# Last 256 tokens as transposed 32x32 blocks, scaled by two engines; the first norm's sums two products later

## The chip, the cores and the metric

The kernel runs on one core of one Trainium2 chip. Time is the device time in microseconds (us) of one execution; lower is better. The core's engines work side by side and wait for each other through semaphores: TensorE (PE, matrix products into PSUM banks), VectorE (DVE), ScalarE (ACT), GpSimd (POOL, hardly used here) and SyncE (SP), whose queue issues the loads and stores.

## What is computed

One decoder layer in fp32 for 1024 tokens of width 1024, then a last norm. Cut to what this change touches:

```python
def rms_norm(x, g):
    xf = x.astype(jnp.float32)
    y = xf * lax.rsqrt(jnp.mean(xf * xf, axis=-1, keepdims=True) + RMS_EPS)
    return (y * g.astype(jnp.float32)).astype(x.dtype)
...
        z = rms_norm(h, norm_mix_g[l])
        proj = z @ w_in[l]
        ...                       # pooling heads, gated recurrence, output projection, MLP
        z = rms_norm(h, norm_ple_g[l])
        gate = jax.nn.sigmoid(z @ w_ple_gate[l] + b_ple_gate[l])
        h = h + gate * (p[l] @ w_ple_proj[l])
    return rms_norm(h, norm_final_g)
```

The output is (1, 1024, 1024).

## The kernel before

Everything lies transposed: 128 of the 1024 channels on the partitions, tokens along the free dimension. `H[0]` to `H[7]` are the eight channel tiles of the residual stream (128 x 1024), `T[0]` to `T[5]` six spare tiles of that size, `R` the inverse root of a norm. A product in fp32 is made of three fp32r products of split operands (high x high, high x low, low x high; helper `mm`, L350), each over at most 512 tokens. A PSUM bank holds 512 columns; there are two pairs of banks and four single ones.

A norm's mean is a sum over channels, that is over partitions: ACT squares each tile, DVE adds the squares up, and PE multiplies them by a matrix of ones (`n_ps`, "the sums", L416 and L417 with split operands `hl`, L426 unsplit). Each row of the result is the same; DVE transposes it in 32x32 blocks so that each of a few columns holds 128 different tokens, ACT takes the root of these columns (`edge`, L438), DVE the reciprocal, and a second transpose of the broadcast columns brings it back to one value a column (L434 to L440, `Norm.rstd`).

The first projection (`ps_l`, three output tiles) goes over the eight input tiles k as they arrive; the norm's factor is multiplied in afterwards, at the eviction (L535). At the last k, the sums of the first norm are placed ahead of that tile's three groups of products. Behind it the loop over the other input projections (`ps_i`), gates (`ps_g`, L571, whose evictions are ACT's L579), pooling and recurrence begins.

At the end comes the gated per-layer input. It goes in four groups of tokens: 0 to 511, 512 to 1023 for channel tiles 2 to 5, then 512 to 767 and 768 to 1023 for the tiles 6, 7, 0, 1. For each channel tile PE makes the gate product (`ps_e`, 24 products) and the projection (`ps_j`, 6); DVE multiplies the gate by `R` (L1045), ACT takes the sigmoid (L1046), DVE multiplies by `ps_j` (L1051) and adds to `H` (L1052); ACT squares the new tile (L389), DVE adds it to the running sum (L390), and ACT multiplies the tile by the last norm's gain (L1081). Tokens 0 to 767 are scaled and stored while products still run (L1071, L1061). For the last 256, the last tile's chain is: gate, sigmoid, product, add, square (L1153), sums, transpose, root, reciprocal, transpose, and then four products of two tiles by the broadcast factor (L1093), each followed by its store (L1094).

The order of work is that of the code as a scheduler places it by its own estimate of times; `pin` (while `in_order` is set) holds an instruction at its place in program order. SP's queue is in order too.

Of the kernel before, what the change touches and what calls it, by code (L numbers as in the profile page):

```python
# [11 lines left out]
ALU = mybir.AluOpType  # L12
# [46 lines left out]
def block_kernel(  # L59
# [65 lines left out]
    def bank(name):  # L125
        return pd.tile([P, HALF], F32, tag="pd", name=name)
# [248 lines left out]
    class Norm:  # L375
# [43 lines left out]
                parts.append((hs, o))  # L419
            return parts  # L420

        def sums_of(self, hs, squares):

            o = bank(f"{self.name}_ps{hs.start}")[:, : hs.stop - hs.start]
            for n, sq in enumerate(squares):
                nc.tensor.matmul(o, ones_f, sq, start=n == 0, stop=n == len(squares) - 1)  # L426
            return [(hs, o)]

        def rstd(self, out, parts=None):


# [92 lines left out]

# [487 lines left out]

    fin = Norm("n3", T[0], T[1:3])
    rfin = T[5]
    gate_p, held, squares = {}, [], [T[0][:, GROUPS[-1]]]
    root = pool.tile([P, 1], F32, name="root")

    def ple_psum(g, hs, o, apart):
# [23 lines left out]
    def ple_out(hs, o, pg, pj, add=True, then=None):  # L1042
        t = T[3 + o % 2][:, : hs.stop - hs.start]
        hv = H[o][:, hs]
        nc.vector.tensor_tensor(by(t, pg), got(pg), by(R[:, hs], pg), ALU.mult)  # L1045
        pin(nc.scalar.activation(t, t, AF.Sigmoid, bias=col("b_ple", o)))  # L1046
        e = t
        if then:
            then(t)
            e = T[3 + (o + 1) % 2][:, : hs.stop - hs.start]  # L1050
        nc.vector.tensor_tensor(by(e, pj), by(t, pj), got(pj), ALU.mult)  # L1051
        nc.vector.tensor_tensor(hv, hv, e, ALU.add)  # L1052
# [27 lines left out]
    def gain(o, hs):  # L1080
        return nc.scalar.activation(H[o][:, hs], H[o][:, hs], AF.Identity, scale=col("g_fin", o))  # L1081

    def finish_last(hs, end, squares):

        fin.rstd(rfin, fin.sums_of(hs, squares))
        gain(end, hs)
        n = hs.stop - hs.start
        done = t_all[:, 1:3].rearrange("p a s -> p (a s)")[:, : NT * n].rearrange("p (o s) -> p o s", o=NT)
        r = rfin[:, hs].unsqueeze(1).broadcast_to([P, 2, n])
        low = end // 2 * 2  # L1090
        for o in [*(o for o in range(0, NT, 2) if o != low), low]:
            os = slice(o, o + 2)
            nc.vector.tensor_tensor(done[:, os], h_all[:, os, hs], r, ALU.mult)  # L1093
            nc.sync.dma_start(out_end[:, os], done[:, os])  # L1094

    END = len(GROUPS) - 1
    for g, hs in enumerate(GROUPS):
        last = len(ORDER[g]) - 1
        if g == END:
            fin.n[hs.start] = len(ORDER[1])  # L1100
        for n, o in enumerate(ORDER[g]):
            end = g == END and n == last
            pg, pj = ple_psum(g, hs, o, end)
            if g == 0 and n < 2:
                ple_gate(g, hs, o, pg, n == 1)
                held.append((o, pg, pj))
                if n == 0:
                    first_sums()
                    continue
                for o, pg, pj in held:  # L1110
                    ple_proj(hs, o, pj)
                for o, pg, pj in held:
                    ple_out(hs, o, pg, pj)
            elif end:
                ple_gate(g, hs, o, pg)
                ple_proj(hs, o, pj)
            else:
                ple_proj(hs, o, pj)
                ple_gate(g, hs, o, pg)
            if g == 0 and 1 <= n < 5:  # L1120
                raw = wp.tile([P, S], F32, tag="raw", name=f"wg0_{n + 3}_raw")
                nc.sync.dma_start(raw, w_gate[n + 3])
                split(raw, *B[n + 3])
                gate_p[n + 3] = B[n + 3]

            if (g > 0 or n > 1) and not end:
                ple_out(hs, o, pg, pj, g < END or n < last - 1)
            if g == 0 and n > 0:
                for o in LATER[n - 1]:
                    ple_in(o, SECOND, norm2)  # L1130
                if n == NT - 2:
                    norm2.rstd(R, norm2.sums((SECOND,)))
            if g == 1:
                gain(o, hs)
                finish(FIRST, DONE[n])
            if g == END - 1:
                gain(o, hs)
            if g == END and n < last - 1:
                gain(o, hs)
            if end:  # L1140
                prev = ORDER[g][n - 1]
                sqs = [T[1 + i][:, hs] for i in range(2)]

                def between(t):

                    pin(nc.scalar.activation(sqs[0], H[prev][:, hs], AF.Square))
                    pin(nc.scalar.activation(root, t[:, :1], AF.Sqrt))
                    pin(gain(prev, hs))

                in_order[:] = [True]  # L1150
                ple_out(hs, o, pg, pj, False, between)
                in_order.clear()
                nc.vector.tensor_tensor(sqs[1], H[o][:, hs], H[o][:, hs], ALU.mult)  # L1153
                squares += sqs
            if g == END:
                finish(GROUPS[END - 1], LAST[n])
    finish_last(GROUPS[-1], ORDER[-1][-1], squares)
    leave("ple")
    leave("proj")

# [72 lines left out]
```

## Time and profile before

| | us |
|---|---|
| median of 3 runs | 927.12 (926.88 to 928.76) |
| profiled execution, its time | 927.23 |
| its span, first to last instruction | 925.4 |
| PE busy | 915.3 (99%) |
| DVE busy | 758.8 (82%) |
| ACT busy | 456.5 (49%) |
| granted PE clock, mean | 0.998 |

In the profile's rows L with a number is a line of the kernel; `out<-in` are the program's names, with buffer numbers left out. PEld is PE's weight load, which runs beside its products. In a list by time a row has its start from the span's first instruction, its length, engine, line, operation, shape and count, and in brackets how long the engine was idle before it and what ended that. Rows of equal instructions that follow each other are merged, and an instruction may start up to 0.1 us before the end of the one ahead when it doesn't need its result.

### The profile page before, as it was taken

The numbers are of one execution on the slowest core, as the hardware profiler recorded it, in microseconds if no ns is written. First come the engines' busy times: TensorE is split into PE (matmuls) and PEld (weight loads), VectorE is DVE, ScalarE is ACT, GpSimd is POOL, SyncE is SP. The second block draws the span as 40 slices with busy tenths as digits, with TensorE's granted clock in tenths as the row PEclk, the third lists the DMA queues.
The fourth block names the chain that finished last, engine by engine and source line by source line (L and its number), as shares of the span: only waits on it lengthen the run. The fifth ranks groups of instructions, "written<-read, shape, count | busy, mean of one in ns | idle before, by whom it ended". The sixth has DMA issues, their size and how long they took to land.

```text
span 925.4 us, 11180 instructions
## 1 busy us (share of the span) xinstructions
PE 915.3 (99%) x4351; PEld 798.5 (86%) x4351; DVE 758.8 (82%) x903; ACT 456.5 (49%) x531; POOL 5.6 (1%) x7
## 2 busy tenths in 40 slices
PE   9999999999999999999999999999999999999996
PEld 7888888888888888888888888888888888888895
DVE  7997985659998888888888989979776679885676
ACT  7567893447543343344334654443444347652544
POOL 0000000002000000000000000000000000000000
PEclk9999999999999999999999999999999999999999
DMA  7210143211244345344534989366532341031022
GB/s 265 99 47 23 46 151 122 69 45 54 84 175 178 125 161 197 142 138 173 191 125 148 341 317 342 110 202 208 188 111 92 118 156 45 16 122 46 1 91 91
DMA packets 45044, 123.97 MB, mean 134 GB/s; under 512 B 4160, under 2 KB 6208, under 8 KB 44992
## 3 DMA queue, kind: packets, MB, share of 16 engines
q1 hardware_dynamic: 44848, 123.22, 38.3%
q8 instruction: 34, 0.56, 0.3%
q14 instruction: 18, 0.15, 0.0%
q10 hardware_dynamic: 144, 0.04, 0.0%
HBM read 89.69 MB, written 33.55 MB: 133 GB/s over the span
## 4 chain that ended last, share of the span: by engine, by line
PE 95%; DVE 2%; issue 1%; DMA 1%; SPq 0%; ACT 0%; DVEq 0%
PE ps_P_d L350 31%; PE ps_P_u L350 31%; PE ps_i L350 10%; PE ps_e L350 10%; PE ps_o L350 9%; PE ps_j L350 1%; DMA h<-in_xT 1%; PE ps_g L571 1%; PE ps_p L350 1%; DVE t L390 1%; PE ps_l L350 0%; DVE wl_lo L179 0%; PE n_ps L417 0%; DVE t L1093 0%; DVE a L182 0%
## 5 line engine op out<-in xcount | busy, mean ns | idle before, releaser
L350 PE MATMUL ps_P_d<-a,wd_P_hi 128*128 128x512 f32 x880 | 261.7, 379 | 0.0
L350 PEld LDWEIGHTS ps_P_d<-a,wd_P_hi 128*128 128x128 f32 x880 | 166.3, 189 | 23.6
L350 PE MATMUL ps_P_d<-a,wd_P_lo 128*128 128x512 f32 x440 | 166.8, 379 | 0.0
L350 PE MATMUL ps_P_u<-a,wu_hi 128*128 128x512 f32 x512 | 152.3, 379 | 0.0
L350 PE MATMUL ps_P_u<-y,wu_hi 128*128 128x512 f32 x384 | 114.2, 379 | 0.0
L350 PEld LDWEIGHTS ps_P_u<-a,wu_hi 128*128 128x128 f32 x512 | 96.8, 189 | 13.8
L350 PE MATMUL ps_P_u<-a,wu_lo 128*128 128x512 f32 x256 | 97.0, 379 | 0.0
L350 PEld LDWEIGHTS ps_P_d<-a,wd_P_lo 128*128 128x128 f32 x440 | 83.2, 189 | 11.8
L350 PEld LDWEIGHTS ps_P_u<-y,wu_hi 128*128 128x128 f32 x384 | 72.6, 189 | 10.4
L747 DVE TENSOR_TENSOR t<-t,ps_P_u 128x512 f32<-128x512 f32 (+1 forms) x80 | 62.6, 782 | 20.4 <-PE ps_P_u L350 20.4
L350 PE MATMUL ps_i<-a,wi_hi 128*128 128x512 f32 x288 | 74.3, 380 | 0.0
L350 PE MATMUL ps_P_u<-y,wu_lo 128*128 128x512 f32 x192 | 72.8, 379 | 0.0
L178 ACT ACTIVATE a<-wd 128x1024 fp32r<-128x1024 f32 x56 | 58.9, 1054 | 21.4 <-PE ps_P_d L350 11.6
L179 DVE TENSOR_TENSOR a<-wd,a 128x1024 fp32r<-128x1024 f32 x56 | 67.2, 1221 | 1.0 <-ACT a L178 0.6
L350 PE MATMUL ps_o<-y,wo_hi 128*128 128x512 f32 x256 | 65.7, 379 | 0.0
L350 PEld LDWEIGHTS ps_i<-a,wi_hi 128*128 128x128 f32 x288 | 54.1, 189 | 8.8 <-issue 1.0
L178 ACT ACTIVATE wu_hi<-wu 128x1024 fp32r<-128x1024 f32 x24 | 25.4, 1057 | 69.8 <-PE ps_P_u L350 44.2
L178 ACT ACTIVATE wu_hi<-wu_raw 128x1024 fp32r<-128x1024 f32 (+1 forms) x26 | 25.2, 974 | 66.3 <-PE ps_P_u L350 41.3
L350 PEld LDWEIGHTS ps_o<-y,wo_hi 128*128 128x128 f32 x256 | 48.4, 189 | 6.8
L350 PEld LDWEIGHTS ps_P_u<-a,wu_lo 128*128 128x128 f32 x256 | 48.4, 189 | 6.8
L178 ACT ACTIVATE wd_P_hi<-wd 128x1024 fp32r<-128x1024 f32 x24 | 25.3, 1054 | 46.9 <-PE ps_P_d L350 46.8
L389 ACT ACTIVATE t<-h 128x512 f32<-128x512 f32 (+2 forms) x44 | 32.0, 731 | 28.3 <-DVE h L1052 20.5
(223 smaller groups left out, 1502.8 us busy)
## 6 DMA issues: line engine op xcount, KB each, us to landing
wd<-act SPq DMA_DIRECT2D x56, 512.0 KB, 5.7
act<-t SPq DMA_DIRECT2D x32, 512.0 KB, 4.3
wu_raw<-in_w_up SPq DMA_DIRECT2D x16, 512.0 KB, 3.4
wu<-in_w_up SPq DMA_DIRECT2D x16, 512.0 KB, 3.9
act<-wu SPq DMA_DIRECT2D x16, 512.0 KB, 4.6
wd<-in_w_down SPq DMA_DIRECT2D x16, 512.0 KB, 6.2
h<-in_xT SPq DMA_DIRECT2D x14, 512.0 KB, 4.4
wg_raw<-in_w_gate SPq DMA_DIRECT2D x10, 512.0 KB, 3.2
```

The source lines that it names most:

```text
L178: first = pin(nc.scalar.activation(hi, src, AF.Copy))
L179: lowest[:] = [pin((eng or nc.vector).tensor_tensor(lo, src, f32(hi), ALU.subtract)).ins]
L350: ins = nc.tensor.matmul(ps, w, turns(z[:, hs]), start=first and z is zhi and w is whi, stop=last and w is wlo, skip_group_check=more,)
L389: pin(nc.scalar.activation(sq, t[:, hs], AF.Square))
L390: self.eng.tensor_tensor(self.acc[:, hs], self.acc[:, hs], sq, ALU.add)
L571: nc.tensor.matmul(x, w[r, o * P : (o + 1) * P], turns(z[r, at : at + HALF]), start=n == 0, stop=n == 2)
L747: (eng or nc.vector).tensor_tensor(to, to if y is None else y, x, ALU.add)
```

## The change

Three things change.

1. **First norm's sums.** At the last input tile, the sums and what follows them stand between the second and the third output tile's products instead of ahead of the first's.
2. **Layout of the last 256 tokens' output.** Instead of multiplying each tile by a factor that differs by column, each tile (already multiplied by the gain) is transposed on DVE in 32x32 blocks, with all tiles' blocks of the same 32 tokens side by side (`turned`). Then a token is a partition within a block, its factor one value a partition, and one instruction scales 32 tokens of all eight tiles (128 x 256). DVE scales blocks 0, 2, 4, 5 and 7, ACT 1, 3 and 6. The second transpose of the factor goes. The host puts the output's blocks back in order when it reshapes. The spare tiles of the squares move from `T[1:3]` to `T[3:5]`, since `T[1]` and `T[2]` now hold the blocks.
3. **The last tile's chain.** From the add on it goes in halves of 128 tokens, with a bank of sums each; the sums of the earlier tiles are made ahead. ACT's square and gain of the tile before stand ahead of the last sigmoid, not behind it. The four stores carry two blocks each, 128 x 512 as before.

The core of the diff:

```diff
-        if k == NT - 1:
-            norm.rstd(R)
...
         for o in range(3):
+            if k == NT - 1 and o == 2:
+                norm.rstd(R)
             mm(ps_l[o], kblk(whi, o), kblk(wlo, o), *A[k], False, k == NT - 1)
...
-    out_end = out[:, NT * S - n_end :].rearrange("p (o s) -> p o s", o=NT)
+    out_end = out[:, NT * S - n_end :].rearrange("p (b x) -> p b x", b=n_end // S * 4)
+    turned_all = t_all[:, 1:3].rearrange("p a s -> p (a s)").rearrange("p (b o j) -> p b o j", o=NT, j=32)
+    turned_flat = t_all[:, 1:3].rearrange("p a s -> p (a s)").rearrange("p (b x) -> p b x", x=32 * NT)
...
-    def finish_last(hs, end, squares):
-
-        fin.rstd(rfin, fin.sums_of(hs, squares))
-        gain(end, hs)
...
-        for o in [*(o for o in range(0, NT, 2) if o != low), low]:
-            os = slice(o, o + 2)
-            nc.vector.tensor_tensor(done[:, os], h_all[:, os, hs], r, ALU.mult)
-            nc.sync.dma_start(out_end[:, os], done[:, os])
+    def turned(o, src=None):
+        src = H[o][:, GROUPS[-1]] if src is None else src
+        return nc.vector.transpose(turned_all[:, :, o], src)
+
+    def ple_last(hs, prev, o, pg, pj):
...
+        in_order[:] = [True]
+        pin(nc.scalar.activation(before, H[prev][:, hs], AF.Square))
+        pin(gain(prev, hs))
+        pin(nc.vector.tensor_tensor(by(t, pg), got(pg), by(R[:, hs], pg), ALU.mult))
+        pin(nc.scalar.activation(t, t, AF.Sigmoid, bias=col("b_ple", o)))
+        pin(nc.scalar.activation(root, t[:, :1], AF.Sqrt))
+        pin(turned(prev))
+        pin(nc.vector.tensor_tensor(by(e, pj), by(t, pj), got(pj), ALU.mult))
+        sums = [bank(f"n3_ps{hs.start}_{i}")[:, :m] for i in range(2)]
+        for x, cut in zip(sums, cuts):
+            for i, sq in enumerate((T[0][:, hs], before)):
+                nc.tensor.matmul(x, ones_f, sq[:, cut], start=i == 0, stop=False)
+        for x, cut in zip(sums, cuts):
+            pin(nc.vector.tensor_tensor(hv[:, cut], hv[:, cut], e[:, cut], ALU.add))
+            pin(nc.vector.tensor_tensor(own[:, cut], hv[:, cut], hv[:, cut], ALU.mult))
+            nc.tensor.matmul(x, ones_f, own[:, cut], start=False, stop=True)
+        pin(nc.scalar.activation(scaled, hv, AF.Identity, scale=col("g_fin", o)))
...
+        def roots(i):
+            r = rfin[:, hs][:, cuts[i]]
+            pin(nc.vector.transpose(r, sums[i]))
+            x = few[:, 4 * i : 4 * i + 4]
+            pin(nc.scalar.activation(x, r.rearrange("p (b t) -> p b t", t=32)[:, :, 0], AF.Sqrt, bias=eps, scale=1.0 / D))
+            return x
...
+        def on_act(b):
+            x = turned_flat[:, b]
+            pin(nc.scalar.activation(x, x, AF.Identity, scale=few[:, b : b + 1]))
+
+        def on_dve(b):
+            x = turned_flat[:, b]
+            pin(nc.vector.tensor_scalar_mul(x, x, few[:, b : b + 1]))
...
+        a = roots(0)
+        pin(turned(o, scaled))
+        inverse(a)
+        on_dve(0)
+        on_act(1)
+        leave_for(slice(0, 2))
+        b = roots(1)
+        on_dve(2)
+        on_act(3)
+        leave_for(slice(2, 4))
+        inverse(b)
+        on_act(6)
+        on_dve(4)
+        on_dve(5)
+        leave_for(slice(4, 6))
+        on_dve(7)
+        leave_for(slice(6, 8))
...
+        if g == 1:
+            fin.tmp = T[3:5]
...
             if g == END - 1:
                 gain(o, hs)
+                turned(ORDER[1][n])
             if g == END and n < last - 1:
                 gain(o, hs)
+                turned(o)
```

**The new order at three places.** A row is the line, the operation, what it writes and reads, and the shape of what it writes.

PE at the first norm, before (`n0_ps` are its sums, `ps_l0` to `ps_l2` the three output tiles at the last input tile):

```order
L350 MATMUL ps_l2_150<-a_70,wl6_lo_379 128x512 x2
L416 MATMUL n0_ps0_420<-hl0_135,ones_142 128x512
L417 MATMUL n0_ps0_420<-hl0_135,ones_142 128x512
L416 MATMUL n0_ps512_425<-hl1_136,ones_142 128x512
L417 MATMUL n0_ps512_425<-hl1_136,ones_142 128x512
L350 MATMUL ps_l0_147<-a_70,wl7_hi_407 128x512 x4
L350 MATMUL ps_l0_147<-a_70,wl7_lo_408 128x512 x2
```

PE there, changed:

```order
L350 MATMUL ps_l1_0_148<-a_70,wl7_lo_408 128x512
L350 MATMUL ps_l1_512_149<-a_70,wl7_lo_408 128x512
L416 MATMUL n0_ps0_432<-hl0_135,ones_142 128x512
L417 MATMUL n0_ps0_432<-hl0_135,ones_142 128x512
L416 MATMUL n0_ps512_437<-hl1_136,ones_142 128x512
L417 MATMUL n0_ps512_437<-hl1_136,ones_142 128x512
L350 MATMUL ps_l2_150<-a_70,wl7_hi_407 128x512 x4
L350 MATMUL ps_l2_150<-a_70,wl7_lo_408 128x512 x2
L350 MATMUL ps_i0_0_486<-a_70,wi0_hi_415 128x512
```

The twelve products of `ps_l0` and `ps_l1` now go first; on DVE the split `wi_lo` moves ahead of the two transposes of the sums.

DVE some 35 us later, in the first pool window (`recip_t` marks its small steps; `y_114` is the low part of the split whose high part ACT makes from the finished window), before:

```order
L622 COPY t<-t 128x1
L631 SCALAR_TENSOR_TENSOR t<-t 128x1023
L179 TENSOR_TENSOR y_131<-h,y_130 128x1024
L629 TENSOR_TENSOR t<-t,recip_t 128x1
L582 TENSOR_TENSOR h<-h 128x1024
L630 TENSOR_TENSOR t<-t 128x1
L179 TENSOR_TENSOR y_114<-t,y_113 128x1024
```

DVE there, changed:

```order
L615 COPY t<-t 128x1
L179 TENSOR_TENSOR y_131<-h,y_130 128x1024
L622 TENSOR_TENSOR t<-t,recip_t 128x1
L624 SCALAR_TENSOR_TENSOR t<-t 128x1023
L623 TENSOR_TENSOR t<-t 128x1
L575 TENSOR_TENSOR h<-h 128x1024
L179 TENSOR_TENSOR y_114<-t,y_113 128x1024
```

The window's last small step (L630, now L623) stands ahead of the product `h<-h` instead of behind it. On ACT one eviction of the gates (64 x 512) moves ahead of a split's high part a little later.

DVE at the end of the program, before:

```order
L1045 TENSOR_TENSOR t<-ps_e_1_6780,rstd 128x256
L1051 TENSOR_TENSOR t<-t,ps_j_1_6781 128x256
L1052 TENSOR_TENSOR h<-h,t 128x256
L1153 TENSOR_TENSOR t<-h 128x256
L434 STREAM_TRANSPOSE t<-n_ps_6820 128x256
L439 RECIPROCAL edge<-edge 128x8
L440 STREAM_TRANSPOSE t<-edge 128x256
L1093 TENSOR_TENSOR t<-h,t 128x512 x4
```

DVE there, changed, from the second half's square on:

```order
L1101 TENSOR_TENSOR t<-h 128x128
L1109 STREAM_TRANSPOSE t<-n_ps_0_6825 128x128
L1076 STREAM_TRANSPOSE t<-t 128x8x32
L1115 RECIPROCAL edge<-edge 128x4
L1123 TENSOR_SCALAR t<-t,edge 128x256
L1109 STREAM_TRANSPOSE t<-n_ps_1_6826 128x128
L1123 TENSOR_SCALAR t<-t,edge 128x256
L1115 RECIPROCAL edge<-edge 128x4
L1123 TENSOR_SCALAR t<-t,edge 128x256 x3
```

The transpose of the broadcast factor and the four products of 512 columns are gone; a transpose into blocks (128x8x32) and five scaled blocks stand there. Ahead of these rows the add and the square stand twice, for 128 columns each, and a block transpose of the tile before follows the last gate eviction.

More of the change, by code (lines that the diff above doesn't have):

```diff
@@ L1040, in ple_proj, with ple_out @@
             mm([(hs, pj)], kblk(wh, o), kblk(wl, o), hi, lo, k == 0, k == len(ple) - 1)
-    def ple_out(hs, o, pg, pj, add=True, then=None):
+    def ple_out(hs, o, pg, pj, add=True):
         t = T[3 + o % 2][:, : hs.stop - hs.start]
@@ L1046, in ple_out @@
         pin(nc.scalar.activation(t, t, AF.Sigmoid, bias=col("b_ple", o)))
[L1047 to L1052, printed above, removed]
+        nc.vector.tensor_tensor(by(t, pj), by(t, pj), got(pj), ALU.mult)
+        nc.vector.tensor_tensor(hv, hv, t, ALU.add)
         if add:
@@ L1081, in gain, with inverse, leave_for @@
         return nc.scalar.activation(H[o][:, hs], H[o][:, hs], AF.Identity, scale=col("g_fin", o))
[L1083 to L1086 removed]
+    def turned(o, src=None):
+        src = H[o][:, GROUPS[-1]] if src is None else src
+        return nc.vector.transpose(turned_all[:, :, o], src)
+    def ple_last(hs, prev, o, pg, pj):
         n = hs.stop - hs.start
[L1088 to L1094 removed]
+        m = n // 2
+        t, e = (T[3 + i % 2][:, :n] for i in (o, o + 1))
+        before, own = (T[3 + i][:, HALF : HALF + n] for i in range(2))
+        scaled = T[3][:, HALF + n :][:, :n]
+        hv = H[o][:, hs]
+        cuts = slice(0, m), slice(m, n)
+        in_order[:] = [True]
[15 more added lines that the diff above has]
+        pin(nc.scalar.activation(scaled, hv, AF.Identity, scale=col("g_fin", o)))
+        few = spread[:, 16:24]
+        def roots(i):
[4 more added lines that the diff above has]
+            return x
+        def inverse(x):
+            pin(nc.vector.reciprocal(x, x))
+        def on_act(b):
[4 more added lines that the diff above has]
+            pin(nc.vector.tensor_scalar_mul(x, x, few[:, b : b + 1]))
+        def leave_for(bs):
+            nc.sync.dma_start(out_end[:, bs], turned_flat[:, bs])
+        a = roots(0)
[15 more added lines that the diff above has]
+        leave_for(slice(6, 8))
+        in_order.clear()
@@ L1137, in block_kernel @@
                 gain(o, hs)
+                turned(ORDER[1][n])
             if g == END and n < last - 1:
                 gain(o, hs)
+                turned(o)
             if end:
[L1141 to L1154, printed above, removed]
+                ple_last(hs, ORDER[g][n - 1], o, pg, pj)
             if g == END:
                 finish(GROUPS[END - 1], LAST[n])
-    finish_last(GROUPS[-1], ORDER[-1][-1], squares)
     leave("ple")
@@ L1230 @@
     out = np.split(np.asarray(r.results[0]["out"]), [NT * GROUPS[-1].start], axis=1)
-    out = np.concatenate([a.reshape(P, NT, -1) for a in out], axis=2)
+    most, end = out[0].reshape(P, NT, -1), out[1].reshape(P // 32, 32, -1, NT, 32)
+    out = np.concatenate([most, end.transpose(0, 4, 3, 2, 1).reshape(P, NT, -1)], axis=2)
     return c(out.transpose(2, 1, 0)).reshape(1, S, D)
```

7 lines of the change are left out of this document (1 added, 6 removed).

## Prediction

> **What bounds the kernel now.** I read the page's shares first, then what TensorE (PE) waited for, then the places of those waits in order of time. In the view of waits a row is: who waited, for whom, microseconds in total, times, longest.
>
> ```profile
> PE 915.3 (99%) x4351; PEld 798.5 (86%) x4351; DVE 758.8 (82%) x903; ACT 456.5 (49%) x531; POOL 5.6 (1%) x7
> ...
> PE ps_l L487 <- DVE heat L367: 1.1, 1, 1.1
> PE n_ps L416 <- DVE hl L414: 0.6, 1, 0.6
> PE n_ps L417 <- DVE hl L415: 0.4, 1, 0.4
> PE n_ps L426 <- DVE t L1153: 0.4, 1, 0.4
> PE n_ps L426 <- ACT t L1146: 0.3, 1, 0.3
> ```
>
> PE is busy 915.3 of 925.4 us and waits, over the whole program, only in three places: at the start, at the sums of the first norm (`n_ps` on L416 and L417), and at the sums of the last 256 tokens (L426). So time can come from two things alone: PE's stall at the first norm, and the tail in which PE has nothing left to do. The change touches exactly these.
>
> **The first norm's sums.** PE in order of time there (start, length, instruction, count, idle before), then VectorE (DVE):
>
> ```profile
> 31.79 1.03 PE L350 MATMUL ps_l<-a,wl_hi 128*128 128x512 f32 x4
> 32.66 0.59 PE L350 MATMUL ps_l<-a,wl_lo 128*128 128x512 f32 x2
> 33.80 0.49 PE L416 MATMUL n_ps<-hl,ones 128*128 128x512 f32 x1 [0.55 <-DVE hl L414]
> 34.74 0.50 PE L417 MATMUL n_ps<-hl,ones 128*128 128x512 f32 x1 [0.44 <-DVE hl L415]
> ...
> 35.68 1.02 PE L350 MATMUL ps_l<-a,wl_hi 128*128 128x512 f32 x4
> ...
> 39.56 1.03 PE L350 MATMUL ps_i<-a,wi_hi 128*128 128x512 f32 x4
> ```
> ```profile
> 34.00 1.29 DVE L415 TENSOR_TENSOR hl<-t,hl 128x512 fp32r<-128x512 f32 x2
> ...
> 35.92 1.18 DVE L179 TENSOR_TENSOR wi_lo<-wi_raw,wi_hi 128x1024 fp32r<-128x1024 f32 x1
> 37.02 0.71 DVE L434 STREAM_TRANSPOSE rstd<-n_ps 128x512 f32<-128x512 f32 x1
> ```
>
> Four products from 31.79 reach 32.66, so one takes 0.217 of PE's time; the two from 32.66 free it at 33.09. The next product of the projection starts at 35.68: the four sums cost 2.59 us. What they cost when nothing is late stands in the chain at a later norm:
>
> ```profile
> 854.67 0.24 PE n2b_ps L416
> 854.91 0.23 PE n2b_ps L417
> ```
>
> That is 0.47 for a half, 0.94 for both, and the stall is worth 2.59 - 0.94 = 1.65 (the 0.55 + 0.44 shown as idle is less, because a stopped stream also loses the overlap of one product's end with the next). In the new order twelve products (`ps_l` 0 and 1, 12 x 0.217 = 2.60) go ahead of the sums, so PE asks for the operands at 33.09 + 2.60 = 35.69. DVE has the last of them at 34.00 + 1.29 = 35.29. No wait is left: gain 1.65.
>
> What is late next? The sums' last result is there at about 35.69 + 3 x 0.235 + 0.50 = 36.90. DVE now does `wi_lo` (1.18) first, from 35.27, then both transposes, and has read the second bank at 37.1 + 0.71 = 37.8. `ps_i` takes those banks, and PE now arrives at 39.56 - 1.65 = 37.91: in time by 0.1. Behind it DVE's first evictions come 0.3 to 0.5 later than now, because ScalarE's (ACT) root waits for the sums, while PE runs 1.65 earlier. Over the next 80 us I looked for the smallest distance between a producer and PE:
>
> ```profile
> 73.33 1.23 DVE L179 TENSOR_TENSOR y<-t,y 128x1024 fp32r<-128x1024 f32 x1 [1.12 <-ACT y L178]
> 80.71 1.06 ACT L178 ACTIVATE y<-t 128x1024 fp32r<-128x1024 f32 x1 [2.81 <-DVE t L630]
> 81.79 1.25 ACT L579 ACTIVATE h<-ps_g,vecs 64x512 f32<-64x512 f32 x2
> ...
> 108.12 1.28 DVE L535 TENSOR_TENSOR t<-ps_i,rstd 128x512 f32<-128x512 f32 x2
> 109.47 1.56 PE L571 MATMUL ps_g<-y,hl 64*128 64x512 f32 x12
> ```
>
> The closest place is the gates at 109.47: the third product (109.8) takes a bank that DVE has just emptied at 108.12 + 1.28 = 109.40, 0.4 before it. If DVE came no earlier, only 0.4 of the 1.65 would be left. But DVE does come earlier: in the new order the 1.2 us product `h<-h` stands between the pool's last small step and the split that waits for ACT, so the idle 1.12 at 73.33 goes (DVE from 0.4 late to 0.7 early); ACT's wait of 2.81 at 80.71 then ends 0.7 earlier and takes in one of the two gate evictions (1.25 / 2 = 0.62) that now follow it. From there both engines are some 1.3 earlier, DVE empties the bank at about 108.1, and PE asks at 109.8 - 1.65 = 108.15. I take off 0.1: **first term -1.55**, bounds -1.65 and -0.4. Later work is released by PE's own products, so the gain stays.
>
> **The tail.** The chain in order of time (start, length), with its last links (between 916.32 and 917.25 stand the add and the square of the last tile, L1052 and L1153, of one length):
>
> ```profile
> 914.86 0.44 DVE t L1045
> ...
> 915.32 0.52 ACT t L1046
> ...
> 916.32 0.43 DVE h L1052
> ...
> 917.25 0.71 PE n_ps L426 x2
> ...
> 917.99 0.46 DVE t L434
> ...
> 918.47 0.32 ACT edge L438
> ...
> 918.81 0.21 DVE edge L439
> ...
> 919.05 0.46 DVE t L440
> ...
> 919.53 0.69 DVE t L1093
> ```
>
> The first store goes out when the first of four DVE products ends, at 920.22. From the stores and from one stretch of them (time; busy of the engines; granted clock, DMA share, GB/s):
>
> ```profile
> L1094 SPq DMA_DIRECT2D out<-t x4: 333/338/345, 920.3 to 922.1; - x4
> DMA to landing us min/median/max: 2.0/2.2/2.3
> 922.00:923.00 1.00, 0.00 (x0) 0.00 (x0) 0.03 (x1) 0.00 (x0) 0.00 (x0) 0.50 1.01 377
> ```
>
> The first lands at 920.29 + 2.0 = 922.3, the last at 922.1 + 2.3 = 924.4, and the span of 925.4 ends 1.0 later. The DMA is full meanwhile: a store is 128 x 512 numbers of 4 bytes, 262 KB, and at 377 GB/s 0.69 long. So a store lands no sooner than 2.0 after its issue and 0.68 after the one before; by this rule the last one lands at 924.3 now.
>
> Up to the product with `ps_j` nothing moves: ACT's square and gain of the tile before now stand ahead of the last sigmoid. Their input is ready at 913.86 + 0.42 = 914.28, they take 0.40 + 0.51, and the sigmoid starts at 915.32 either way. The rows for this and for the next prices:
>
> ```profile
> 913.86 0.42 DVE L1052 TENSOR_TENSOR h<-h,t 128x256 f32<-128x256 f32 x1
> ...
> 915.73 0.40 ACT L1146 ACTIVATE t<-h 128x256 f32<-128x256 f32 x1
> 916.15 1.28 ACT L1147 ACT_TABLE_LOAD   x1
> 917.55 0.89 ACT L1081 ACTIVATE h<-h,vecs 128x256 f32<-128x256 f32 x2
> ```
> ```profile
> 904.25 0.29 DVE L414 CAST ple<-t 128x256 fp32r<-128x256 f32 x1
> 912.18 0.43 DVE L1045 TENSOR_TENSOR t<-ps_e,rstd 128x256 f32<-128x256 f32 x1 [0.72 <-PE ps_e L350]
> ```
>
> From 916.32 on, with halves. DVE takes 0.69 at 512 and 0.42 at 256 columns, so 0.29 at 128: add 916.32 to 916.61, square 916.64 to 916.93, the second half's add to 917.14 and square to 917.46. PE's half sum takes 0.71 now and between 0.35 and 0.71 with half the columns; a part of it is fill, so 0.5: DVE can transpose it at 917.48, done 917.80 (0.32 by the same slope from 0.46 and 0.71). Meanwhile ACT loads its table (now directly behind the sigmoid, 915.85 to 917.13), takes the tiny root, and scales the last tile by the gain, 917.25 to 917.76. Root of the first half 917.83 to 918.14; under it DVE turns the scaled tile, 917.79 to 918.24; reciprocal to 918.37. The second transpose of the old chain (0.46) is gone. Then both engines scale a block each: ACT 918.41 to 918.92 (0.51), and the **first store goes at 918.98, 1.31 earlier**. The second follows ACT's next block at 919.75 (second half's root 918.96 to 919.27, block to 919.69), the third behind DVE's block 5 at 920.13, the fourth at 920.5. Landings by the rule above: 921.0, 921.75, 922.4, 923.1 against 924.3: **second term -1.2**. Each store now waits for two engines instead of one, but behind it in SP's queue stand only the later stores, none of which is ready before it.
>
> The price that no row shows is DVE's product of a tile with a column of scalars, five of them. Bounds: the product of two tiles, 0.43 (row at 912.18), and the cast of one tile, 0.29 (row at 904.25). I take 0.29, since this too reads one tile; with 0.43 the fourth store goes at 920.8, the last landing is 923.2 and the term -1.1. On this the Trainium skill (VectorE: DVE Perf Modes, § The perf-mode tier table) says that fp32 `tensor_scalar` from SBUF runs at twice the rate of `tensor_tensor`, which needs both read ports; by it the term is -1.2, and by a plain reading of the 0.43 row it is -1.1. The two rows agree with it so far (0.29 for one tile, 0.43 for two); no scaled block has run here.
>
> A transpose into blocks 1 KB apart is not in the trace either: eight of them, two on the path (the tile before the last, whose window is 915.29 to 915.86, and the last one). Bounds: 0.45, the 256-column transpose as it stands, and 0.71, that of twice the columns; I take 0.45 for equal element counts. With 0.71 the path is 0.06 + 0.26 longer. The other six stand before them, where DVE waits now and then (0.72 at 912.18, which makes good the one just ahead of the third group's stores) and PE, by the view of waits, for nobody. The squares of the sums move to two tiles that are dead by then, at no cost. With all unknowns at their dear end, half sum included, the term is -0.5; at the cheap end -1.3, where the first store's 1.31 is kept to the last.
>
> **Sum.** -1.55 - 1.2 = -2.75 on the profiled execution's 927.23 gives 924.5; the median of the runs, 927.12, is 0.11 below it, so **924.4**, 0.29% faster. 0.2% (1.85 us) is about what a measurement of this kernel can tell from no change.
>
> **Rivals.** (1) The norm's gain is eaten at the gates: DVE and ACT don't catch up after 73, and PE waits at 109.8 for the bank, so that 0.4 is left: 927.12 - 0.4 - 1.2 = 925.5. For it speaks that DVE starts its evictions later and shows no idle before 73.33; against it the idle 1.12 and 2.81, which the new order fills. (2) The tail gives nothing: strided transposes at 1.2 us each add 0.55 and 0.75 to the path: 925.6. Against it: the same number of elements. (3) Slower: the same mechanism further on. With x for one transpose the path grows by (x - 0.65) + (x - 0.45), and only when 2x - 1.1 passes 2.75 + 1.85, x = 2.85, is the kernel slower by 0.2%; at x = 3.0, 929.3. That would be six times the row at 917.99.
>
> **Chances.** The forecast 0.73, (1) 0.13, (2) 0.09, (3) 0.05. Faster by over 0.2% is below 925.27: the forecast nearly whole (0.70), and the milder ends of (1) and (2), together 0.78; within 0.2% 0.17; slower 0.05. The range reaches down to both terms at their cheap ends (927.12 - 1.65 - 1.3 = 924.2) less 0.5 for the spread of runs, 923.7, and up over (1) and (2) with 0.3, 925.9.
>
> **What would show it.** Right: no wait of PE on `hl` at L416/L417, `ps_i` starting near 37.9, gates near 107.8, PE's last product near 913.9, the first store 4.1 us after the last gate eviction (5.4 now), landings 0.7 apart. Wrong: a PE wait on the transposes' banks near 38 or on `t<-ps_i` near 108; block transposes well over 0.45; scaled blocks over 0.42 on DVE; a first store near 919.5 on the old axis.

## Result and profile after

| | before | after |
|---|---|---|
| median of 8 runs each, us | 927.38 (926.88 to 928.89) | 924.57 (924.31 to 925.52) |
| ratio to before, 95% interval | | 0.9969 (0.996 to 0.9978) |
| span of the profiled execution, us | 925.4 | 922.8 |
| first `ps_i` product | 39.56 | 37.90 |
| `ps_i` behind the gates near 108 | 110.97 | 109.53 |
| last gate eviction starts (`t<-ps_e`) | 914.86 | 913.40 |
| first of the four last stores issued | 920.29 | 917.49 |

The changed kernel is 0.31% faster. Between two profiled executions the last gate eviction splits the gain: 1.46 us lie ahead of it (the first norm), and 9.4 us instead of 10.6 follow (the tail). The shares of the engines and what PE waited for, in the profile after:

```profile
PE 914.6 (99%) x4357; PEld 798.6 (87%) x4357; DVE 760.6 (82%) x915; ACT 459.1 (50%) x535; POOL 5.8 (1%) x7
...
PE ps_l L480 <- DVE heat L367: 1.1, 1, 1.1
PE n_ps L1102 <- DVE t L1101: 0.6, 1, 0.6
```

The waits on `hl` are gone, and the wait in the tail is one on the half's square. PE in order of time at the first norm (start, length, instruction):

```profile
33.09 1.03 PE L350 MATMUL ps_l<-a,wl_hi 128*128 128x512 f32 x4
...
35.68 0.40 PE L416 MATMUL n_ps<-hl,ones 128*128 128x512 f32 x1
...
36.61 1.02 PE L350 MATMUL ps_l<-a,wl_hi 128*128 128x512 f32 x4
...
37.90 1.03 PE L350 MATMUL ps_i<-a,wi_hi 128*128 128x512 f32 x4
```

From 35.68 to 36.61 the four sums take 0.93 (2.59 before). `ps_i` starts 1.66 earlier and finds its banks free, since VectorE has read both by 36.44 + 1.31 = 37.75:

```profile
36.44 1.31 DVE L427 STREAM_TRANSPOSE rstd<-n_ps 128x512 f32<-128x512 f32 x2
...
72.69 1.23 DVE L179 TENSOR_TENSOR y<-t,y 128x1024 fp32r<-128x1024 f32 x1
...
106.91 1.28 DVE L528 TENSOR_TENSOR t<-ps_i,rstd 128x512 f32<-128x512 f32 x2
```
```profile
107.82 1.78 PE L564 MATMUL ps_g<-y,hl 64*128 64x512 f32 x12
109.53 1.13 PE L350 MATMUL ps_i<-a,wi_hi 128*128 128x512 f32 x4
```

At 72.69 VectorE no longer waits for ScalarE (1.12 before), and it is 1.21 earlier at 106.91. That is less than PE's 1.65: the bank is empty at 108.19, and the twelve gate products with what follows take 109.53 - 107.82 = 1.71 instead of 1.50. So 0.2 of the 1.66 is lost here, and nothing more until the last gate eviction (1.46 there). The chain of the tail in order of time, and then the four stores with the last row of that line's view (from issue to landing):

```profile
913.40 0.43 DVE t L1090
...
914.86 0.30 DVE h L1100
...
915.19 0.30 DVE t L1101
...
915.53 0.50 PE n_ps L1102 x2
...
916.06 0.32 DVE t L1109
916.37 0.39 DVE t L1076
916.76 0.17 DVE edge L1115
...
916.96 0.35 DVE t L1123
```
```profile
917.49 0.34 SPq L1126 DMA_DIRECT2D out<-t  x1
...
918.29 0.34 SPq L1126 DMA_DIRECT2D out<-t  x1
...
919.23 0.38 SPq L1126 DMA_DIRECT2D out<-t  x1
...
DMA to landing us min/median/max: 2.1/2.2/2.5
```

The first store goes 917.49 - 913.40 = 4.09 after the last gate eviction (5.43 before). The last goes 5.83 after it (7.20 before) and takes 2.5 to land, since the earlier ones are still being moved: the last three land at 920.37, 921.04 and 921.71, 0.67 apart.

### The profile page after: what moved, and what is told of

It is laid out like the page before. It is cut to its first block, busy times and chain, and to the rows that moved or that the text cites. A ratio compares the mean times of both kernels' runs of the same rounds, so it can differ in the third digit from the quotient of the medians.

```text
span 922.8 us, 11209 instructions
## 1 busy us (share of the span) xinstructions
PE 914.6 (99%) x4357; PEld 798.6 (87%) x4357; DVE 760.6 (82%) x915; ACT 459.1 (50%) x535; POOL 5.8 (1%) x7
## 4 chain that ended last, share of the span: by engine, by line
PE 98%; DMA 1%; DVE 0%; SPq 0%; ACT 0%; issue 0%; DVEq 0%
PE ps_P_u L350 31%; PE ps_P_d L350 31%; PE ps_i L350 10%; PE ps_e L350 10%; PE ps_o L350 9%; PE ps_l L350 3%; PE ps_j L350 1%; PE ps_g L564 1%; DMA h<-in_xT 1%; PE ps_p L350 1%; PE n_ps L417 0%; PE n_ps L416 0%; DVE t L1123 0%; SPq L486 0%; DVE a L182 0%; ACT a L181 0%
```

## Experiments

One caution for reading them. Kernels with the same order of work on PE up to the first norm still start `ps_i` at different times, as in the run with the chain uncut and in the one with eight stores (both below):

```profile
37.52 0.38 PE L350 MATMUL ps_i<-a,wi_hi 128*128 128x512 f32 x1
```
```profile
38.45 0.38 PE L350 MATMUL ps_i<-a,wi_hi 128*128 128x512 f32 x1
```

Spans of single executions are therefore not compared. What is compared is the medians (of at least five runs, against runs of the kernel before taken beside them), and two distances inside each trace: how much longer than in the kernel before it takes from the `ps_i` group at 98.92 to the one at 110.97 (the loss at the gates), and how long after the start of the last gate eviction the first store is issued and the span ends. The table is worked out from the traces before rounding; labels are those of the expectations.

| kernel | median, us | against before (us; ratio and interval) | loss at the gates | first store | end of span |
|---|---|---|---|---|---|
| before | | | 0 | 5.43 | 10.58 |
| after | 924.57 | -2.81; 0.9969 (0.996 to 0.9978) | 0.22 | 4.09 | 9.38 |
| norm_only | 925.67 | -1.51; 0.9983 (0.9974 to 0.9992) | 0.18 | 5.43 | 10.59 |
| tail_only | 925.92 | -1.26; 0.9986 (0.9977 to 0.9995) | 0 | 4.09 | 9.37 |
| sums_after_first | 925.71 | -1.47; 0.9985 (0.9976 to 0.9994) | 0.72 | 4.09 | 9.37 |
| sums_after_third | 925.13 | -2.05; 0.998 (0.9971 to 0.9988) | 0 | 4.09 | 9.37 |
| evict_again | 924.92 | -2.18; 0.9975 (0.9965 to 0.9986) | 0.79 | 4.09 | 9.38 |
| evict_soon | 924.36 | -2.74; 0.997 (0.9958 to 0.9981) | 0 | 4.08 | 9.37 |
| first_evict_soon | 924.59 | -2.51; 0.9972 (0.9961 to 0.9984) | 0 | 4.08 | 9.36 |
| tail_whole | 925.17 | -1.93; 0.9979 (0.997 to 0.9988) | 0.19 | 4.73 | 9.90 |
| blocks_on_dve | 924.64 | -2.54; 0.9971 (0.996 to 0.9982) | 0.20 | 4.20 | 9.45 |
| store_each_block | 925.01 | -2.17; 0.9977 (0.9968 to 0.9986) | 0.20 | 3.94 | 9.90 |
| five_and_evict | 924.56 | -2.62; 0.9968 (0.9956 to 0.9981) | 0 | 3.94 | 9.26 |
| turn_twice | 925.01 | -2.10; 0.9977 (0.9968 to 0.9986) | 0.20 | 4.47 | 9.75 |

### Each part alone

The kernel before with only the sums moved:

```diff
-        if k == NT - 1:
-            norm.rstd(R)
...
         for o in range(3):
+            if k == NT - 1 and o == 2:
+                norm.rstd(R)
```

> The kernel before with one edit: the first norm's sums stand ahead of the third group of the projection's last block; the tail is the old one. Theory (first term whole, 1.65 gained at the sums and 0.2 lost again at the gates near 108): the first ps_i product starts near 37.9, the last gate eviction comes 1.45 earlier than in the kernel before (914.86 to about 913.4), span 924.0, time -1.45 us (ratio 0.9984). Rival (the gain is eaten at the gates): only 0.4 is left, last eviction near 914.5, span 925.0. Rival (the changed kernel's gain is all tail): no change.

The changed kernel with that one edit undone:

```diff
+        if k == NT - 1:
+            norm.rstd(R)
...
         for o in range(3):
-            if k == NT - 1 and o == 2:
-                norm.rstd(R)
```

> The changed kernel with the first norm's sums put back to their old place, so that the new tail stands alone. Theory (second term -1.2, independent of the first): the last gate eviction at 914.86 as in the kernel before, first store 4.1 after it (5.43 before), last landing 8.3 after it (9.5 before), span 924.2, time -1.2 us (ratio 0.9987). Rival (the tail gives nothing, all 2.6 come from the norm): first store 5.4 after the eviction, no change in time. With the run of the norm alone, the two gains must add up to the 2.6 of the changed kernel's span if the terms are independent.

Measured: -1.51 and -1.26 us. They add up to -2.77, and the whole change gives -2.81; but each of the three has an interval of about 0.8 us either side, so the sum alone shows little. The traces show more: the norm alone has the same small loss at the gates (0.18) and the old tail to 0.01 us; the tail alone has no loss at the gates and the new tail (9.37). So neither part disturbs the other, and each has about the size predicted. The rival in which the norm is eaten down to 0.4 at the gates and the one in which the tail gives nothing both fall.

The size of the stall that is removed is less certain than one trace makes it look. The kernel with the tail alone keeps the old order at the first norm, and its PE waits less there:

```profile
32.77 0.59 PE L350 MATMUL ps_l<-a,wl_lo 128*128 128x512 f32 x2
...
34.33 0.50 PE L417 MATMUL n_ps<-hl,ones 128*128 128x512 f32 x1 [0.44 <-DVE hl L415]
...
35.27 1.03 PE L350 MATMUL ps_l<-a,wl_hi 128*128 128x512 f32 x4
```

PE is free at 32.77 + 2 x 0.217 = 33.20 and goes on at 35.27. The four sums cost 2.07 there instead of 2.59, and the stall is 2.07 - 0.94 = 1.13 instead of 1.65.

### Where the sums stand

```diff
-            if k == NT - 1 and o == 2:
+            if k == NT - 1 and o == 1:
                 norm.rstd(R)
```

> The changed kernel with the sums one group earlier, ahead of the second group: only six products of 0.217 us (1.30) lie ahead of them, so PE asks for the operands at 33.09 + 1.30 = 34.39, while VectorE has the last of them at 35.29. Theory (what is gained is the cover of products ahead of the sums): the last two sums wait, some 0.3 to 0.5 of the 1.65 are lost at that place (first ps_i near 38.3); the gates then ask later and lose nothing there (0.2 less lost), so at the tail it is 0.1 to 0.3 later than the changed kernel, time -2.3 to -2.5 us against before. Rival (any place after the first products frees the stall alike): first ps_i at 37.9 as in the changed kernel.

Measured: -1.47 us in place of -2.3 to -2.5. The loss at the sums was as foreseen: the four sums and their waits take PE from 34.82 to 36.21, 1.39 instead of 0.94. What was not foreseen is the rest, at the gates. VectorE and then PE there:

```profile
73.53 1.23 DVE L179 TENSOR_TENSOR y<-t,y 128x1024 fp32r<-128x1024 f32 x1 [1.12 <-ACT y L178]
...
108.32 1.28 DVE L528 TENSOR_TENSOR t<-ps_i,rstd 128x512 f32<-128x512 f32 x2
```
```profile
109.15 1.85 PE L564 MATMUL ps_g<-y,hl 64*128 64x512 f32 x12 [0.36 <-DVE t L528]
110.93 1.13 PE L350 MATMUL ps_i<-a,wi_hi 128*128 128x512 f32 x4
```

Here VectorE waits 1.12 for ScalarE at 73.53, as in the kernel before, and evicts at 108.32 instead of 106.91; the product `h<-h`, which fills that gap in the changed kernel, stands at 68.79 there. PE, which comes earlier than before, now waits for it, and 0.72 is gone. This is the first rival of the prediction, alive in a neighbouring order.

```diff
         for o in range(3):
-            if k == NT - 1 and o == 2:
-                norm.rstd(R)
             mm(ps_l[o], kblk(whi, o), kblk(wlo, o), *A[k], False, k == NT - 1)
+        if k == NT - 1:
+            norm.rstd(R)
```

> The changed kernel with the sums one group later, behind all three groups. Theory (what is late next is the banks: ps_i takes the sums' banks, which VectorE's transposes read first; in the changed kernel they are free 0.1 before PE asks): the sums end near 37.9 without a wait, VectorE reads the two banks by about 38.9 and 39.5, and PE waits there for the transposes, 1.0 to 1.7 us; first ps_i products near 39 to 39.5, and of the norm's 1.65 at most 0.6 is left: time -1.2 to -1.8 us against before, all but the tail lost. Rival (the banks are no limit, other banks are free or the transposes come at once): no wait, first ps_i at 37.9, time as the changed kernel, -2.6.

Measured: -2.05 us. A wait on the banks is there, but a smaller one:

```profile
37.65 1.31 DVE L427 STREAM_TRANSPOSE rstd<-n_ps 128x512 f32<-128x512 f32 x2 [1.37 <-PE n_ps L417]
```
```profile
38.52 0.67 PE L350 MATMUL ps_i<-a,wi_hi 128*128 128x512 f32 x2 [0.44 <-DVE rstd L427]
```

PE would have started `ps_i` at 37.92 (the last sum starts at 37.69 and occupies PE for 0.23) and starts at 38.52: 0.6 lost, not 1.0 to 1.7. The expectation let VectorE wait for all four sums; in fact it turns the first half while PE still sums the second. At the gates nothing is lost, as VectorE's order is another one here and it starts that eviction at 105.26, with the gates at 108.50. So in these three traces the place between the second and the third group loses least, 0.2 in all: one group earlier PE waits for the operands (0.45) and at the gates (0.72), one group later for the banks (0.6). The medians stand in the same order, but neighbouring intervals overlap.

### What the gates wait for

An extra eviction of the first half, ahead of the gates:

```diff
     ps = project(4)
     lru_gates(2)
+    normed(T[0], ps[:1])
     normed(T[0], ps)
```

> The changed kernel with one extra instruction on VectorE: the first half of the window input (t<-ps_i, 128x512) that stands ahead of the gates near 108 is evicted a second time, behind both halves, 0.6 us more before its bank is free. The rest is untouched. In the changed kernel the gates start at 107.82 and the next ps_i follows 1.71 later (1.50 in the kernel before), so 0.21 is lost there. Theory (the gates wait there for the bank that VectorE empties, nothing else): the loss grows by the 0.6 to about 0.8, next ps_i at 110.1, everything behind it 0.6 later, time -2.2 us against the kernel before. Rival (the 0.21 is something else, ScalarE or the length of the products): no change, -2.8.

The same eviction scheduled earlier on VectorE:

```diff
     ps = project(4)
     lru_gates(2)
-    normed(T[0], ps)
+    with tc.high_priority(200):
+        normed(T[0], ps)
```

> The changed kernel with that eviction (both halves) scheduled earlier on VectorE, ahead of one split of the pool's output and of the split of the next weights; it then ends near 105.9 instead of 108.19. Theory (the bank sets the gates): the gates take 1.50 again, next ps_i at 109.32, the whole 1.65 of the norm reaches the tail: last gate eviction 13.20 after 900 instead of 13.40, time -0.2 us against the changed kernel, -3.0 against the kernel before. Rival: the gates take 1.71 as in the changed kernel, or what was moved back (the weights' split) delays the next ps_i by up to 1.

And the last edit applied to the kernel with the sums after the first group:

> The sums after the first group (where 0.72 of the gain was lost at the gates near 109, since VectorE keeps there the order of the kernel before and evicts at 108.32 instead of 106.91), with the eviction scheduled earlier as in the run named evict_soon. Theory (the loss at the gates is VectorE's order between 73 and 108, not the place of the sums as such): no wait at the gates, the gain at the tail is what stands at the first ps_i, 0.4 less than in the changed kernel with the same edit: time about -2.2 to -2.6 against the kernel before, 0.7 to 1.1 better than the sums after the first group alone. Rival (the place of the sums delays VectorE's chain by itself): the gates still wait, time -1.5 as without the edit.

VectorE and PE in order of time, first with the extra eviction, then with the earlier one:

```profile
107.22 1.88 DVE L528 TENSOR_TENSOR t<-ps_i,rstd 128x512 f32<-128x512 f32 x3
...
108.65 1.85 PE L564 MATMUL ps_g<-y,hl 64*128 64x512 f32 x12 [0.43 <-DVE t L528]
110.43 0.92 PE L350 MATMUL ps_i<-a,wi_hi 128*128 128x512 f32 x3
```
```profile
104.44 1.28 DVE L528 TENSOR_TENSOR t<-ps_i,rstd 128x512 f32<-128x512 f32 x2
...
107.65 1.56 PE L564 MATMUL ps_g<-y,hl 64*128 64x512 f32 x12
109.15 1.13 PE L350 MATMUL ps_i<-a,wi_hi 128*128 128x512 f32 x4
```

0.6 us more on VectorE raise the loss from 0.22 to 0.79, and the median by 0.6 (-2.18 against -2.81). With the eviction over at 105.72 the gates take 1.50 again and the loss is 0. The same edit takes the whole 0.72 out of the kernel with the sums after the first group, and its median goes from -1.47 to -2.51. That is 1.04, more than the 0.72, and its trace shows where some of the rest may lie: the sums hardly wait there either.

```profile
34.30 0.40 PE L416 MATMUL n_ps<-hl,ones 128*128 128x512 f32 x1
...
35.35 1.03 PE L350 MATMUL ps_l<-a,wl_hi 128*128 128x512 f32 x4
```

They take 1.05 instead of 1.39, with the same order of work up to there. So what the early place costs at the sums differs from one trace to another, and with the earlier eviction the places after the first and after the second group (-2.51 and -2.74) cannot be told apart. The loss at the gates, in turn, is VectorE's eviction of the bank: a longer one raises it, and an earlier one removes it in two kernels. How much it costs hangs on VectorE's order between 73 and 108. On the median the 0.2 of evict_soon cannot be told from the changed kernel.

### The tail taken apart

Without halves:

```diff
-        cuts = slice(0, m), slice(m, n)
+        cuts = (slice(0, n),)
...
-        sums = [bank(f"n3_ps{hs.start}_{i}")[:, :m] for i in range(2)]
+        sums = [bank(f"n3_ps{hs.start}_{i}")[:, :n] for i in range(1)]
...
-            x = few[:, 4 * i : 4 * i + 4]
+            x = few
...
-        b = roots(1)
...
-        inverse(b)
```

> The changed kernel with the chain behind the last product not in halves: one add, one square, one sum, one transpose, one root and one reciprocal over the 256 columns; blocks, engines and stores as in the change. Theory (the halves shorten the chain by what the second half of each link takes, and the stores follow the first block): add to 915.29, square to 915.75, sum to 916.50, transpose to 916.98, reciprocal to 917.60, first store at 918.15 instead of 917.49 (+0.66), then 0.5 apart, last landing +0.5: time +0.5 us against the changed kernel, -2.3 against the kernel before. Rival (the end is set by the stores' transfer alone, which is the same 1 MB): first store later, last landing the same, +0.1 at most. Rival (a half costs as much as a whole, so that cutting only adds instructions): faster than the changed kernel by 0.3.

The chain, and the first store, which follows the last gate eviction (at 913.02 there) by 4.73:

```profile
914.93 0.43 DVE t L1101
...
915.41 0.71 PE n_ps L1102 x2
...
916.15 0.46 DVE t L1109
...
916.98 0.21 DVE edge L1115
```
```profile
917.75 0.34 SPq L1126 DMA_DIRECT2D out<-t  x1
```

Square, sum and transpose have the lengths of a whole again (0.43, 0.71 and 0.46 against 0.30, 0.50 and 0.32). First store +0.64, end +0.52, median +0.88 against the -2.81 of the changed kernel, of which the trace shows 0.52 in the tail. The halves are worth 0.5 us, as expected; the other 0.36 stands against an interval of 0.8 us either side in the medians' ratio and is left open.

All blocks on VectorE (shown for two; the others likewise, in the order 0 to 7):

```diff
-        on_act(1)
+        on_dve(1)
...
-        on_act(3)
+        on_dve(3)
```

> The changed kernel with all eight blocks of the last 256 tokens scaled by VectorE, ScalarE idle there. A block takes VectorE about 0.31 us in the changed kernel and ScalarE 0.45 to 0.51. Theory (two engines are worth what VectorE must take over): first store at 917.62 instead of 917.49, second near 918.5, third 919.35, fourth 919.95 instead of 919.23; last landing 922.0 to 922.1 instead of 921.71: +0.3 to +0.4 us against the changed kernel. Rival (VectorE alone keeps up with the stores, 0.62 for two blocks against 0.68 for the transfer of one store): +0.1 at most.

```profile
918.20 1.14 DVE L1123 TENSOR_SCALAR t<-t,edge 128x256 f32<-128x256 f32 x4
...
919.37 0.33 SPq L1126 DMA_DIRECT2D out<-t  x1
...
DMA to landing us min/median/max: 2.0/2.1/2.2
```

Measured: the end only 0.07 later, where 0.3 to 0.4 was expected; the rival holds. VectorE takes 1.14 / 4 = 0.285 for a block in a row of them, two blocks 0.57, less than the 0.68 in which a store is moved. The last store is issued 0.36 later than in the changed kernel (6.18 after the last gate eviction against 5.83) but lands after 2.2 instead of 2.5; the stores are issued farther apart there, so it seems to queue less. ScalarE's share of the scaling is worth next to nothing here.

Eight stores:

```diff
         on_dve(0)
+        leave_for(slice(0, 1))
         on_act(1)
-        leave_for(slice(0, 2))
+        leave_for(slice(1, 2))
...
         on_dve(7)
-        leave_for(slice(6, 8))
+        leave_for(slice(7, 8))
```

> The changed kernel with eight stores of one block (131 KB) each instead of four of two, each issued when its block is done. Theory (SyncE needs 0.43 us for an issue and 0.47 from one to the next, which is longer than the 0.34 that 131 KB take to move): first store at 917.33 instead of 917.49, but the eighth at about 920.6 instead of the fourth at 919.23; its landing 1.7 later, near 922.3 instead of 921.71: +0.6 us against the changed kernel. Rival (the DMA sets the end, finer stores only start it earlier): last landing near 921.5, -0.2.

SyncE's last stores there, and the view of that line:

```profile
920.26 0.40 SPq L1126 DMA_DIRECT2D out<-t  x1
...
920.75 0.40 SPq L1126 DMA_DIRECT2D out<-t  x1
...
921.24 0.40 SPq L1126 DMA_DIRECT2D out<-t  x1
...
DMA to landing us min/median/max: 1.7/1.8/1.9
```

Each of the last four issues follows the one before by 0.49, though the last block is ready at 919.53 (the earlier gaps lie between 0.39 and 0.54). The last one is issued 921.24 - 913.93 = 7.31 after the last gate eviction, 1.5 later than in the changed kernel, and the end is 0.52 later. Finer stores start the transfer 0.15 sooner and then make SyncE the bound.

Five stores and the earlier eviction together:

```diff
         on_dve(0)
+        leave_for(slice(0, 1))
         on_act(1)
-        leave_for(slice(0, 2))
...
         on_dve(2)
+        leave_for(slice(1, 3))
         on_act(3)
-        leave_for(slice(2, 4))
+        leave_for(slice(3, 4))
```

> The changed kernel with two edits: the window input ahead of the gates near 108 evicted earlier (as in the run named evict_soon), and five stores instead of four, the first of block 0 alone, then 1 and 2, then 3, then two and two. Theory: 0.2 from the gates; first store 0.16 earlier (917.33 on the axis of the changed kernel), SyncE's 0.47 between issues still hidden, no hole in the transfer, last landing 0.15 earlier: -0.35 us against the changed kernel, -3.1 against the kernel before. Rival (the fifth issue or the smaller first store costs what the early start brings): only the 0.2 of the gates, -2.9.

The trace shows both gains: no loss at the gates, and 9.26 from the last gate eviction to the end (9.38 in the changed kernel). The median, -2.62, does not show them; 0.3 us of 924 is less than these runs can tell.

The block transpose of the last tile twice in a row:

```diff
         pin(turned(o, scaled))
+        pin(turned(o, scaled))
         inverse(a)
```

> The changed kernel with the block transpose of the last tile done twice in a row (128x256 into 32x32 blocks 1 KB apart, 0.45 us in the changed kernel, between the first half's transposed sum and its reciprocal). Theory (the transpose is on the path that sets the end, as the slower rival of the prediction assumed, and its price is 0.4 to 0.45): first store 4.5 after the last gate eviction starts instead of 4.09, last landing and the end of the span 0.4 later too (9.8 after that eviction instead of 9.38): time +0.4 us against the changed kernel. Rival (it lies beside the root on ScalarE and the transfer of the stores takes up the rest): first store later, the end by less than 0.1.

```profile
918.35 0.93 DVE L1076 STREAM_TRANSPOSE t<-t 128x256 f32<-128x256 f32 x2
```

One more transpose of 0.45 moves the first store by 0.38 and the end by 0.37. So the last tile's transpose is on the path, at the price of a plain one of its size. For this one of its two transposes the prediction's slower rival had the mechanism right and the price six times too high.

## Why the prediction was right, point by point

- **The first term**, -1.55 (bounds -1.65 and -0.4): -1.51 when run alone (interval -0.7 to -2.4), -1.46 between the two traces. No wait on `hl`, sums in 0.93, `ps_i` at 37.90 (37.91 forecast), banks read at 37.75 (37.8 forecast). "What is late next" was the gates, as written: the wait of 1.12 at 73 went, ScalarE's wait at 80 shrank from 2.81 to 2.10, and VectorE had the bank free at 108.19 (108.1 forecast). The mis-sized piece is the 0.1 taken off there: it is 0.2. That single times are met to 0.01 to 0.1 is luck: the stall was 1.13 in another trace of the old order, and the first `ps_i` starts anywhere between 37.52 and 38.45 in traces of the new one. What is shown is the mechanism, and the size to about half a microsecond.
- **How near rival (1) was**: its mechanism is real, shown by adding and by removing the eviction's delay. In the order with the sums one group earlier it takes 0.72. It cost so little in the changed kernel because the product `h<-h` stands ahead of the split that waits for ScalarE, as the prediction's working had it; this is read from the two orders, no run moved that product alone.
- **The second term**, -1.2 (bounds -0.5 and -1.3): -1.20 in the trace, -1.26 alone. First store 4.09 after the last gate eviction (4.1 forecast), last landing 8.31 after it (923.1 - 914.86 = 8.24 forecast); the landings are 0.82, 0.67 and 0.67 apart.
- **Its unknown prices**: the half sum 0.50 (taken as 0.5), the block transpose 0.44 to 0.45 (0.45), the scaled block 0.35 where it stands alone and 0.285 in a row (0.29, bounds 0.29 and 0.43). The Trainium skill (VectorE: DVE Perf Modes, § The perf-mode tier table) puts fp32 `tensor_scalar` from SBUF at twice the rate of `tensor_tensor`. The direction agrees, the factor is not reached at this size: a block alone takes 0.35, the product of two tiles of this size 0.43. For its bounds of the block transpose the prediction took 0.65 as hidden without deriving it, where its own window, 915.29 to 915.86, is 0.57; at 0.45 this changes nothing.
- **What the second term is made of** was not asked in the prediction. The halves are worth 0.52 of the 1.20. The other 0.68, with the 0.07 of the second engine in it, is what the kernel without halves keeps (its end is at 9.90 against 10.58), and rows show where it lies, though no run took it apart: from the end of the reciprocal to the first store it takes 917.75 - 917.19 = 0.56, where the kernel before takes 920.29 - 919.02 = 1.27. The second transpose, 0.46, is gone from there, and a block stands where a product of 512 columns (0.69) stood.
- **The sum**: -2.75 forecast, -2.81 between the medians and -2.66 between the two spans before rounding. The forecast of 924.4 stood on the earlier median of 927.12; beside 927.38 in the same runs the difference is met to 0.06. That is far closer than the interval of about 0.8 us either side can tell, so the last tenths are luck.
- **What failed was in the experiments' expectations**: that the gates lose nothing when the sums stand one group earlier (VectorE's order changed with their place), that the bank's transposes start only after all four sums, and that VectorE alone would be late with the blocks.

## What to carry to other kernels

When a stall on the bounding engine is removed, look for the next producer it runs into and how far that one is itself pulled along; a scheduler can answer a moved piece with another order tens of microseconds later, so read that order and don't assume the old one. In a tail that ends in stores, shorten the chain to the first store, then compare three rates for the rest: what scales a block, what issues a store (0.4 to 0.5 us here) and what moves it (0.68 us for 262 KB). Here the transfer set the end with four stores (scaling every block on one engine moved it by 0.07), and the issue with eight (0.52).

## What the runs showed beside

- **The start is not fixed.** In nine kernels with the same order of work on PE up to there (the changed one among them), the first `ps_i` product starts between 37.52 and 38.45; in the latest three PE waited for the split of `x` (0.3 to 0.9 us in all) on ScalarE and VectorE. The one with the norm alone starts at 38.10 without such a wait, so the cause of the spread stays open. Kernels that differ by a few tenths can't be told apart by one span.
- **A late reload cost 2 us once.** In the profiled execution of turn_twice ScalarE waits for the down weights, and PE behind it; of the other traces none loses more than 0.3 in that stage:

```profile
549.11 1.06 ACT L178 ACTIVATE a<-wd 128x1024 fp32r<-128x1024 f32 x1 [5.08 <-DMA wd<-act]
...
555.80 0.48 PE L350 MATMUL ps_P_d<-a,wd_P_lo 128*128 128x512 f32 x1 [1.43 <-DVE wd_P_lo L179]
```

- **A store's fixed part.** With nothing queued ahead, 131 KB land 1.74 us after the start of the issue and 262 KB 2.03 to 2.08, so 131 KB cost 0.29 to 0.34 (385 to 452 GB/s) and the fixed part is some 1.4. The Trainium skill (DMA: Bandwidth & Descriptors, § Anatomy of one DMA) gives 2.0 us plus the bytes at 436 GB/s, fitted to transfers issued from GpSimd. The slope agrees as far as these times tell; the fixed part of these stores from SyncE is some 0.6 smaller.
